# The opening's token sums and query weight sums on GpSimd, and query results turned by VectorE

## The chip, the cores and the metric

The kernel runs on one core of a Trainium2 chip. The metric is the device time of one execution in microseconds (us). Before the change three runs gave 1890.53, 1891.34 and 1893.8 us; the median is 1891.34.

## The reference

One decoder layer over 2048 tokens of width 1024, in float32. All branches start from one projection of the normed input:

```python
h = rms_norm(x, norm_g)
u = jnp.einsum('bsd,dc->bsc', h, w_in)
v_c, b_c, c_c, z_c, q, k, v, z_a, gate_logits = jnp.split(u, SPLIT_POINTS, axis=-1)
...
q = rms_norm(q.reshape(b, s, N_Q_HEADS, HEAD_DIM), q_norm_g)
k = rms_norm(k.reshape(b, s, N_KV_HEADS, HEAD_DIM), k_norm_g)
...
return x + jnp.einsum('bsd,de->bse', merged, w_out)
```

Branch A is a gated causal convolution of width 3, branch B a sliding-window attention (window 128, 16 query heads of 64 over 4 key heads) with sinks. The two are projected, merged with sigmoid gates and projected once more. For this change two things matter: the product of `h` with the query columns of `w_in`, and the mean square of each query head, which the norm of `q` needs.

## The kernel before, in words

The tokens are worked on in two tiles of 1024 (tile one is `t == 0`). Every projection is cut into units: two blocks of 128 columns by 1024 tokens, summed over 1024 inputs. Each float32 operand is held as a high and a low part, so a product of two operands takes three matmuls per pair of input chunks, twelve matmuls over the four pairs. ScalarE makes the high part (a cast), VectorE the low part (operand less high part).

**Units of seven products.** A unit (`sunit`, L494) does not form its eight block products one by one. It uses seven products of sums, in the order 1, 5, 6, 2, 7, 3, 4. The token operand of each is one of eight "forms" (`oph_m_j` in the order's rows: form m of input pair j, j from 0 to 3). Forms 1, 2, 3 and 8 are plain quarters of the normed input. Forms 5, 6, 7 and 4 are made of sums: `first_sum` overwrites the even chunk's left half (form 5), `second_sum` overwrites it again (form 6), `third` overwrites the even chunk's right half (form 7), `last_sum` writes a tile of its own, `t` (form 4). A sum may only overwrite what the form before has read, and a form may only be split after its sum. There are 16 such sums, of 128 x 512 elements, in the opening. The weights are treated in the same way (`sums`, L388): four sums per unit make the halves that products 5 and 6 (`wq_sh`, `wq_sl`) and 7 and 3 (`wq_th`, `wq_tl`) use, in place in the raw weights, after the plain half (`wq_ah`, `wq_al`) and the single (`wq_d`) have been split off. Product 6 adds onto a copy of product 1, which ScalarE writes into the bank Y (L503).

**The opening.** TensorE first makes keys and values by token, then the query units q0, q1, q2, q3, then the convolution's units. q0 has no sums: it uses forms 1, 2, 8 and 3 in plain products (`qunit`, L531), which gives VectorE time to make the others. q1 is the first unit with seven products.

**What a query result goes through** (`fin_q`, L808). A result is copied to `q_t`, scaled and split (`q_h`, `q_l`), and sent by GpSimd to memory in four transfers (`q2d`). For its mean square it is turned so that a head's elements lie along a row, squared by ScalarE, and summed up by VectorE. Where `BY_PE` holds a 1, TensorE turns it (`turn4`, the matmuls of L708: four transposes of 128 x 128 into a bank `ptq`) and the whole head lies in one row, 8 sums a result. Where it holds a 0, VectorE turns it in blocks of 32 x 32 into the bank (16 sums a result), and `squares_sum` adds the two halves of a head with four small copies and four small adds per unit. Before, q0, q1 and q2 of tile one are turned by TensorE and q3 by VectorE; in tile two VectorE turns all.

**What sets the order.** The order is written out in the program. `run` (L684) issues one product, then the work that `put` has placed at this tick: ScalarE's and VectorE's share of a weight piece, the steps of the tables `OP_X` to `OP_S`, results to evacuate. VectorE's instructions go through `vec`, a helper which also takes a step of waiting chains after each instruction, so all of them carry line L262. Each engine takes its own instructions strictly in order. GpSimd, besides, issues the transfers `vd` (values), `kd` (keys), `q2d` (queries), and later the attention's.

**The k transposes.** TensorE turns the normed keys of the first tile into banks `pbk` (L766), between products. These share a ring of three banks with `ptq`.

Of the kernel before, what the change touches and what calls it, by code (L numbers as in the profile page):

```python
# [60 lines left out]
Q_PARTS = [1, 4, 4, 0]  # L61
Q_SUMS = [8, 7, 6, 3]
ROOT = (1, 1, 1, 0)
BY_PE = [1, 1, 1, 0]
OP_X = [1, 1, 1, 6, 7, 7, 8, 11]
OP_P = [3, 2, 3, 4, 4, 4, 5, 6]
OP_L = [7, 8, 6, 6, 8, 7, 9, 7]
# [38 lines left out]
def block_kernel(  # L106
# [12 lines left out]
    nc = tc.nc  # L119
# [18 lines left out]
    def slot(shape, dt, name):  # L138
        return big.tile(shape, dt, tag="big", name=name)
# [160 lines left out]
    def add(o, a, b, eng=None):  # L300
        return (eng or vec).tensor_tensor(out=o, in0=a, in1=b, op=ALU.add)

    def sub(o, a, b, eng=None):
        return (eng or vec).tensor_tensor(out=o, in0=a, in1=b, op=ALU.subtract)
# [45 lines left out]
    def wpair(name):  # L350
        return [wpool.tile([P, KP * UC], F32R, tag="w", name=f"{name}{i}") for i in "hl"]

    def pieces_of(n):

        kind, srcs, key = plan[n]
        name = "w" + "_".join(str(i) for i in key)
        w = {}

        def two(hi, lo, src):
            return (lambda: nc.scalar.copy(hi, src),  # L362
                    lambda: vec.tensor_tensor(
                        out=lo, in0=src, in1=hi.bitcast(F32), op=ALU.subtract))

        if kind == "R":
            return w, []

        if kind:
            def pair(h, m1, m2, nm):  # L370
                hi, lo = (v.rearrange("p (i j c) -> p i j c", i=2, c=P) for v in wpair(f"{name}_{nm}"))
                for i, m in enumerate((m1, m2)):
                    w[m] = (hi[:, i], lo[:, i])
                return two(hi, lo, raws[2 * n + h])

            if kind == "P":
                return w, [(2, 1, lambda h=h: pair(h, (h, 0), (h, 1), f"p{h}")) for h in range(2)]

            def single():
                if n in paired:  # L380
                    hl = [slot([P, KP, P], F32R, f"{name}_d{i}") for i in "hl"]
                else:
                    d = wpool.tile([P, 2, KP, P], F32R, tag="w", name=f"{name}_d")
                    hl = [d[:, 0], d[:, 1]]
                w[4] = tuple(hl)
                return two(*hl, raws[2 * n + 1][:, 1])

            def sums():  # L388
                ra, rb = raws[2 * n], raws[2 * n + 1]

                def f():
                    sub(ra[:, 0], ra[:, 0], rb[:, 0])
                    summed.append(vec.chain(
                        lambda: add(rb[:, 0], rb[:, 0], rb[:, 1]),
                        lambda: sub(rb[:, 1], rb[:, 1], ra[:, 0]),
                        lambda: sub(ra[:, 1], ra[:, 1], rb[:, 1])))

                return (lambda: None, f)

            summed = []  # L400

            def of_sums(*args):
                summed[0]()
                return pair(*args)

            def single_sums():
                hi, lo = single()
                _, f = sums()

                def g():  # L410
                    lo()
                    f()

                return hi, g

            first = [(1, 0, single), (0, 0, sums)] if n not in paired else [(0, 0, single_sums)]
            return w, [(2, 0, lambda: pair(0, 1, 2, "a")), *first,
                       (2, 1, lambda: of_sums(1, 5, 6, "s")), (2, 1, lambda: of_sums(0, 7, 3, "t"))]
# [225 lines left out]
    def third(c, st):  # L644

        raw = st["raw"]
        sub(raw[c - 1, 1], raw[c, 1], raw[c - 1, 1])

    def norm_r(t, c, st):

# [2 lines left out]
    def first_sum(j, st):  # L653

        raw = st["raw"]
        sub(raw[2 * j, 0], raw[2 * j, 1], raw[2 * j, 0])

    def second_sum(j, st):

        raw = st["raw"]  # L660
        sub(raw[2 * j, 0], raw[2 * j + 1, 1], raw[2 * j, 0])

    def last_sum(j, st, to=None):

        raw = st["raw"]
        o = st.setdefault("t4", {})[j] = raw[2 * j, 0] if to is None else to
        sub(o, raw[2 * j + 1, 0], raw[2 * j, 0])

    def form(t, m, j, st):
        raw = st["raw"]  # L670
# [137 lines left out]
    def fin_q(t, j):  # L808
        by_pe = t == 0 and BY_PE[j]
        ss = small.tile([P, 32 if by_pe else 64], F32, tag="ss" if by_pe else "ss4", bufs=3 if by_pe else 2, name=f"qss{t}_{j}")  # L810
# [631 lines left out]
    for t in range(NT):  # L1442
# [9 lines left out]
        for word in (SEQ0, SEQ1)[t].split():  # L1452
            both_ = word.split("+")
            for name in both_:
                if len(both_) > 1:
                    paired.add(len(plan))
                key, j = name.rstrip("0123456789"), int(name[-1]) if name[-1].isdigit() else None
# [26 lines left out]
    raw, ops, xs = st["raw"], st["ops"], st["x"]  # L1484
# [77 lines left out]
    def t4(j):  # L1562
        last_sum(j, st, slot([P, H], F32, f"t4_{j}"))
# [24 lines left out]
    rights(0)  # L1588
    forms(1)
    each(0, lambda j: first_sum(j, st))  # L1590
    forms(2)
    rights(1)
    each(1, lambda j: second_sum(j, st))
    forms(3)
    forms(4)
    each(2, lambda j: third(2 * j + 1, st))
    forms(5)
    each(3, t4)
# [165 lines left out]
```

## Time and profile before

| | |
|---|---|
| runs | 1890.53, 1891.34, 1893.8 us |
| profiled execution | 1890.92 us, span 1889.2 us, clock 1.0 |
| TensorE busy | 1880.8 us |
| VectorE busy | 1540.0 us |
| ScalarE busy | 989.0 us |
| GpSimd busy | 728.7 us |

In the profile PE is TensorE (PEld its weight loads), DVE VectorE, ACT ScalarE, POOL GpSimd. A row of the order of time has the start and the length in us, engine, line, operation, what is written and read, and a count; square brackets tell what ended an idle time before it. A row by tile has the shortest, median and longest length in ns. A group's row has the busy time in all and the mean of one in ns. Matmuls overlap, so their pace is read from start to start. The difference between the execution and its span, 1.7 us, lies outside the program's instructions.

### The profile page before, as it was taken

The numbers are of one execution on the slowest core, as the hardware profiler recorded it, in microseconds if no ns is written. First come the engines' busy times: TensorE is split into PE (matmuls) and PEld (weight loads), VectorE is DVE, ScalarE is ACT, GpSimd is POOL, SyncE is SP. The second block draws the span as 40 slices with busy tenths as digits, with TensorE's granted clock in tenths as the row PEclk, the third lists the DMA queues.
The fourth block names the chain that finished last, engine by engine and source line by source line (L and its number), as shares of the span: only waits on it lengthen the run. The fifth ranks groups of instructions, "written<-read, shape, count | busy, mean of one in ns | idle before, by whom it ended". The sixth has DMA issues, their size and how long they took to land.

```text
span 1889.2 us, 27869 instructions
## 1 busy us (share of the span) xinstructions
PE 1880.8 (100%) x8638; PEld 1565.5 (83%) x8638; DVE 1540.0 (82%) x2536; ACT 989.0 (52%) x1993; POOL 728.7 (39%) x1038
## 2 busy tenths in 40 slices
PE   9999999999999999999999999999999999999999
PEld 7888888888888888888887888888888888888887
DVE  7989888789878889887579988888877789887654
ACT  7665554567665345435455645556566436344321
POOL 1472454456667111021075445656666311121000
PEclk9999999999999999999999999999999999999999
DMA  8475566689888978889367557768888869899653
GB/s 307 123 217 170 144 175 190 182 246 302 251 246 258 318 267 301 286 286 296 112 184 221 182 170 207 206 164 238 243 241 255 269 245 347 318 281 272 223 173 110
DMA packets 261189, 435.81 MB, mean 231 GB/s; under 512 B 33649, under 2 KB 124785, under 8 KB 261041
## 3 DMA queue, kind: packets, MB, share of 16 engines
q1 hardware_dynamic: 202848, 314.13, 50.3%
q0 software_dynamic: 58048, 119.87, 24.0%
q8 instruction: 69, 1.13, 0.3%
q14 instruction: 80, 0.65, 0.1%
q10 hardware_dynamic: 144, 0.03, 0.0%
HBM read 279.48 MB, written 154.42 MB: 230 GB/s over the span
## 4 chain that ended last, share of the span: by engine, by line
PE 82%; issue 7%; DVE 5%; DMA 3%; POOL 2%; ACT 1%; SPq 0%; POOLq 0%; DVEq 0%; ACTq 0%
PE Y L480 30%; PE Vcv L480 5%; PE Xcv L480 5%; PE po L1118 2%; PE Xgb L480 2%; PE Xb L480 2%; PE Vgb L480 2%; PE Xz L480 2%; PE Vb L480 2%; PE Vz L480 2%; PE Vo L480 2%; PE Xo L480 2%; PE Xza L480 2%; PE Vza L480 2%; PE Vga L480 2%
## 5 line engine op out<-in xcount | busy, mean ns | idle before, releaser
L1080 POOL DMA_DIRECT2D x<-fd x256 | 144.1, 614 | 69.7 <-DMA fd<-f 24.9
L1101 POOL TENSOR_SCALAR_AFFINE_SELECT xh<-xh 64x512 fp32r<-64x512 f32 x64 | 66.7, 1043 | 133.1 <-DVE xl L262 96.2
L1053 ACT ACTIVATE p<-s,st,rq 128x128 f32<-128x128 f32 x256 | 113.0, 451 | 5.7 <-DMA fd<-f 3.7
L1073 POOL DMA_DIRECT2D fd<-f x64 | 39.0, 610 | 176.6 <-DVE f L262 152.3
L480 PE MATMUL Xcv<-oph,wcv_ah 128*128 128x512 f32 x256 | 79.5, 392 | 0.0
L1134 POOL DMA_DIRECT2D od<-o x64 | 69.4, 1092 | 24.6 <-DMA od<-o 20.4
L855 POOL DMA_DIRECT2D q2d<-q_h x64 | 44.3, 692 | 84.3 <-ACT q_h L850 81.9
L1324 POOL DMA_DIRECT2D md<-thyb x32 | 27.4, 872 | 103.3 <-DVE thyb L262 87.7
L1101 POOL TENSOR_SCALAR_AFFINE_SELECT xl<-xl 64x512 fp32r<-64x512 f32 x64 | 64.3, 1004 | 4.4
L1101 POOL TENSOR_SCALAR_AFFINE_SELECT yp<-yp 64x512 fp32r<-64x512 f32 x64 | 55.7, 870 | 5.0 <-ACT yp L1088 0.9
L1101 POOL TENSOR_SCALAR_AFFINE_SELECT yp<-xl 64x512 fp32r<-64x512 f32 x64 | 56.1, 876 | 3.1
L480 PEld LDWEIGHTS Xcv<-oph,wcv_ah 128*128 128x128 f32 x256 | 47.3, 188 | 9.4
L262 DVE SCALAR_TENSOR_TENSOR y<-u,cols,y 128x512 f32<-128x512 f32 x64 | 51.5, 804 | 3.7 <-ACT y L1163 2.5
L262 DVE TENSOR_TENSOR p<-p,st 128x512 f32<-128x512 f32 x64 | 49.7, 776 | 2.6
L262 DVE TENSOR_TENSOR opa<-ina,opa 128x512 fp32r<-128x512 f32 x56 | 36.2, 686 | 18.3 <-ACT opa L297 18.3
L1053 ACT ACTIVATION_READ_ACCUMULATOR p<-s,st,rq 128x1 f32 x256 | 50.9, 199 | 0.0
L362 ACT CAST wcv_sh<-wcv_raw 128x1024 fp32r<-128x1024 f32 x16 | 16.8, 1053 | 63.5 <-DVE wcv_raw L262 63.5
L480 PE MATMUL Xcv<-oph,wcv_al 128*128 128x512 f32 x128 | 49.8, 389 | 0.0
L855 POOL DMA_DIRECT2D q2d<-q_l x64 | 44.1, 689 | 12.6 <-DVE q_l L262 9.9
L1028 PEld LDWEIGHTS s<-kq,q 128*128 128x128 f32 x256 | 45.9, 189 | 2.2
L262 DVE STREAM_TRANSPOSE f<-p 128x512 f32<-128x512 f32 x64 | 45.4, 710 | 2.7 <-DVE p L262 0.2
L262 DVE TENSOR_TENSOR opc<-inc,opc 128x512 fp32r<-128x512 f32 x56 | 36.1, 686 | 13.9 <-ACT opc L297 13.8
(774 smaller groups left out, 6611.5 us busy)
## 6 DMA issues: line engine op xcount, KB each, us to landing
wcv_raw<-in_w_in SPq DMA_DIRECT2D x32, 512.0 KB, 4.2
q<-q2d SPq DMA_DIRECT2D x64, 256.0 KB, 4.7
v<-vd SPq DMA_DIRECT2D x128, 128.0 KB, 4.7
fd<-f POOLq DMA_DIRECT2D x64, 256.0 KB, 3.8
x<-fd POOLq DMA_DIRECT2D x256, 64.0 KB, 3.6
gd<-th SPq DMA_DIRECT2D x64, 256.0 KB, 3.4
wq_raw<-in_w_in SPq DMA_DIRECT2D x16, 512.0 KB, 5.0
q2d<-q_h POOLq DMA_DIRECT2D x64, 128.0 KB, 3.7
```

The costliest lines, as they stand in the source:

```text
L262: r = f(*args, **kw)
L362: return (lambda: nc.scalar.copy(hi, src), lambda: vec.tensor_tensor(out=lo, in0=src, in1=hi.bitcast(F32), op=ALU.subtract))
L480: nc.tensor.matmul(ps, lhsT=w[:, j, :], rhs=b[:, m, :], start=start and j == 0 and i == 0, stop=j == KP - 1 and i == 2, skip_group_check=n ...
L855: nc.gpsimd.dma_start(q2d[t][j][half, q * 2 * HB : (q + 1) * 2 * HB, i, e, :], src[HALVES[e]].bitcast(F32).rearrange("p (b x) -> p b x", x ...
L1028: nc.tensor.matmul(sp[:, h, c, skip : 3 * HD], lhsT=q2[:, h, c, :], rhs=kq[:, 0, keys], start=False, stop=c == 1)
L1053: nc.scalar.activation(out=p[:, i, :], in_=sg[:, i, HD : 3 * HD], func=AF.Exp, bias=st[:, 1, i : i + 1], scale=rv[:, i // 2, i % 2 : i % 2 ...
L1073: nc.gpsimd.dma_start(fd, f)
L1080: nc.gpsimd.dma_start(x[QUADS[k]], src[k])
L1101: nc.gpsimd.affine_select(out=d4, in_=s4, pattern=[[0, 2], [-32 * sg, 2], [0, G], [-sg, 32]], compare_op=ALU.is_gt if prev else ALU.is_ge, ...
L1118: nc.tensor.matmul(po[:, cs], lhsT=v2[:, kind, :], rhs=xx[:, :, h * HD : (h + 1) * HD], start=h == 0 and n == 0, stop=n == 2, skip_group_c ...
L1134: put(tick[0] + ADD_WAIT, lambda: nc.gpsimd.dma_start(to, o[UH].rearrange("p c e q -> p (c e) q"), accum_op=ALU.add))
L1324: nc.gpsimd.dma_start(md[t][k, :, hs(q)], m, accum_op=ALU.add)
```

## The change

`BY_PE` becomes 0 for all four query units of tile one, so that VectorE turns their results. The sums on tokens in the opening (`first_sum`, `second_sum`, `third`, `last_sum`) and the four weight sums of q1, q2 and q3 are issued on GpSimd instead of VectorE. The weight sums of the other units stay on VectorE. No table of ticks changes. ScalarE's order up to product 6 of q1 is the same as before.

```diff
-BY_PE = [1, 1, 1, 0]
+BY_PE = [0, 0, 0, 0]
...
                 def f():
+                    if key[0] == "q" and key[1] == 0:
+                        eng = nc.gpsimd
+                        sub(ra[:, 0], ra[:, 0], rb[:, 0], eng)
+                        add(rb[:, 0], rb[:, 0], rb[:, 1], eng)
+                        sub(rb[:, 1], rb[:, 1], ra[:, 0], eng)
+                        sub(ra[:, 1], ra[:, 1], rb[:, 1], eng)
+                        summed.append(lambda: None)
+                        return
                     sub(ra[:, 0], ra[:, 0], rb[:, 0])
...
     def third(c, st):
-        sub(raw[c - 1, 1], raw[c, 1], raw[c - 1, 1])
+        sub(raw[c - 1, 1], raw[c, 1], raw[c - 1, 1], nc.gpsimd)
...
     def first_sum(j, st):
-        sub(raw[2 * j, 0], raw[2 * j, 1], raw[2 * j, 0])
+        sub(raw[2 * j, 0], raw[2 * j, 1], raw[2 * j, 0], nc.gpsimd)
...
     def second_sum(j, st):
-        sub(raw[2 * j, 0], raw[2 * j + 1, 1], raw[2 * j, 0])
+        sub(raw[2 * j, 0], raw[2 * j + 1, 1], raw[2 * j, 0], nc.gpsimd)
...
     def last_sum(j, st, to=None):
-        sub(o, raw[2 * j + 1, 0], raw[2 * j, 0])
+        sub(o, raw[2 * j + 1, 0], raw[2 * j, 0], nc.gpsimd)
```

GpSimd's queue before, from the first query result's last transfers to the third result's first; `xt` are the token chunks, `q_0_1_0` is query unit 0, block 1, token half 0:

```order
L855 DMA q2d_0_92<-q_0_0_0_l 64x8x64
L747 DMA vd<-v_4_765 64x4x128 x2
L747 DMA vd<-v_5_770 64x4x128 x2
L855 DMA q2d_0_92<-q_0_1_0_h 64x8x64
L855 DMA q2d_0_92<-q_0_1_0_l 64x8x64
L855 DMA q2d_0_92<-q_0_1_0_h 64x8x64
L855 DMA q2d_0_92<-q_0_1_0_l 64x8x64
L855 DMA q2d_0_92<-q_0_0_1_h 64x8x64
```

The same place after the change, as far as the second sum of pair two, in front of its form 6 (`xt_156` is the even chunk of pair zero, `xt_169` of pair two, `xt_176` of pair three; of two rows that read alike the first is the third sum, for form 7, the other the second sum, for form 6):

```order
L304 TENSOR_TENSOR xt_156<-xt_160,xt_156 128x512
L755 DMA vd<-v_4_765 64x4x128 x2
L755 DMA vd<-v_5_770 64x4x128 x2
L304 TENSOR_TENSOR xt_156<-xt_160,xt_156 128x512
L304 TENSOR_TENSOR t_1_792<-xt_165,xt_163 128x512
L863 DMA q2d_0_92<-q_0_1_0_h 64x8x64
L863 DMA q2d_0_92<-q_0_1_0_l 64x8x64
L863 DMA q2d_0_92<-q_0_1_0_h 64x8x64
L863 DMA q2d_0_92<-q_0_1_0_l 64x8x64
L304 TENSOR_TENSOR xt_169<-xt_172,xt_169 128x512
L304 TENSOR_TENSOR xt_176<-xt_179,xt_176 128x512
L304 TENSOR_TENSOR xt_169<-xt_172,xt_169 128x512
```

The token sums now stand between the transfers of values and queries, each of which waits for a split by VectorE. Ahead of this piece stand six token sums, the four weight sums of q1 and the four transfers of the first query result.

GpSimd's queue before, where the transfers of q1's last result end (`k_1_1` and `k_0_1` are parts of the keys):

```order
L855 DMA q2d_1_93<-q_1_1_0_h 64x8x64
L855 DMA q2d_1_93<-q_1_1_0_l 64x8x64
L776 DMA kd_100<-k_1_1_h 64x2x512
L776 DMA kd_100<-k_1_1_l 64x2x512
L776 DMA kd_100<-k_1_1_h 64x2x512
L776 DMA kd_100<-k_1_1_l 64x2x512
L776 DMA kd_100<-k_0_1_h 64x2x512
```

The same place after the change:

```order
L863 DMA q2d_1_93<-q_1_1_0_h 64x8x64
L863 DMA q2d_1_93<-q_1_1_0_l 64x8x64
L784 DMA kd_100<-k_1_1_h 64x2x512
L784 DMA kd_100<-k_1_1_l 64x2x512
L784 DMA kd_100<-k_1_1_h 64x2x512
L784 DMA kd_100<-k_1_1_l 64x2x512
L304 TENSOR_TENSOR wq_3_raw_892<-wq_3_raw_892,wq_3_raw_894 128x512
L301 TENSOR_TENSOR wq_3_raw_894<-wq_3_raw_894 128x512
L304 TENSOR_TENSOR wq_3_raw_894<-wq_3_raw_894,wq_3_raw_892 128x512
L304 TENSOR_TENSOR wq_3_raw_892<-wq_3_raw_892,wq_3_raw_894 128x512
L784 DMA kd_100<-k_0_1_h 64x2x512
```

The four weight sums of q3 stand behind 24 issues that follow the sums of q2: four `vd`, sixteen `q2d` of q1 and four `kd`.

VectorE's rows before, in front of the last forms 6 (product 6 of q1 reads them):

```order
L262 TENSOR_TENSOR xt_176<-xt_179,xt_176 128x512
L262 TENSOR_TENSOR xt_169<-xt_172,xt_169 128x512
L262 TENSOR_TENSOR xt_176<-xt_179,xt_176 128x512
L262 TENSOR_TENSOR oph_7_1_848<-xt_163,oph_7_1_848 128x512
L262 TENSOR_TENSOR oph_7_2_851<-xt_169,oph_7_2_851 128x512
L262 TENSOR_TENSOR t_2_854<-xt_172,xt_169 128x512
L262 SCALAR_TENSOR_TENSOR q_0_0_1_l<-q_0_0_1_t,gqk,q_0_0_1_h 128x512
```

And after:

```order
L262 TENSOR_TENSOR wq_1_sl<-wq_1_raw_302,wq_1_sh 128x1024
L262 TENSOR_TENSOR oph_7_1_848<-xt_163,oph_7_1_848 128x512
L262 TENSOR_TENSOR oph_7_2_851<-xt_169,oph_7_2_851 128x512
L262 SCALAR_TENSOR_TENSOR q_0_0_1_l<-q_0_0_1_t,gqk,q_0_0_1_h 128x512
L262 TENSOR_REDUCE kss_1_709<-ksq_3_828 128x8
```

The sums are gone from between the splits; what the splits read now comes from GpSimd.

## The prediction

> **What bounds the kernel now.** I read the page first, then the opening by stretches of 25 us.
>
> ```profile
> span 1889.2 us, 27869 instructions
> PE 1880.8 (100%) x8638; PEld 1565.5 (83%) x8638; DVE 1540.0 (82%) x2536; ACT 989.0 (52%) x1993; POOL 728.7 (39%) x1038
> 50.00:75.00 25.00, 25.00 (x112) 20.72 (x111) 24.65 (x45) 16.02 (x30) 7.94 (x12) 1.00 0.25 66
> 100.00:125.00 25.00, 25.00 (x125) 20.84 (x124) 19.92 (x36) 14.64 (x26) 18.40 (x29) 1.00 0.81 222
> ```
>
> TensorE never rests, so whatever it no longer does shortens the run and whatever makes it wait lengthens it. The second number of a stretch is TensorE's busy time, then the weight loads', VectorE's, ScalarE's and GpSimd's. VectorE is full at 50 to 75 us (24.65 of 25) and GpSimd has room (7.94); at 100 to 125 us it is GpSimd that is the busier of late (18.40), all of it the issuing of transfers. Next, TensorE's order of time, with and without a turn of a query result:
>
> ```profile
> 92.74 2.88 PE L480 MATMUL Y<-oph,wq_d 128*128 128x512 f32 x12
> 95.46 0.60 PE L708 MATMUL ptq<-ident,q_t 128*128 128x128 f32 x4
> 95.81 0.71 PE L480 MATMUL Xq<-oph,wq_ah 128*128 128x512 f32 x2
> 98.65 0.62 PE L480 MATMUL Vq<-oph,wq_sh 128*128 128x512 f32 x2
> 63.26 0.62 PE L545 MATMUL Qq<-oph,wq_p0h 128*128 128x512 f32 x2
> 79.94 1.03 PE L480 MATMUL Y<-oph,wq_sh 128*128 128x512 f32 x2
> 120.87 0.71 PE L480 MATMUL Vq<-oph,wq_sh 128*128 128x512 f32 x2
> ```
>
> A product of 12 matmuls alone takes 95.46 - 92.74 = 2.72 us, a turn with the product behind it 98.65 - 95.46 = 3.19. The last three rows are dates that I need: form 8 is first wanted at 63.26, form 6 at 79.94 (its first pair takes 0.32 longer than the 0.71 usual behind a transpose: it waits already now, for VectorE's forms), the weight sums of q2 at 98.65 and of q3 at 120.87.
>
> **Part 1: turns off TensorE.** 12 turns (three q units of four) at 3.19 - 2.72 = 0.47: **-5.6 us**. TensorE has no idle time for them to have hidden in. VectorE gets 12 transposes instead:
>
> ```profile
> 144.24 0.72 DVE L262 STREAM_TRANSPOSE ptq<-q_t 128x512 f32<-128x512 f32 x1
> L262 DVE TENSOR_TENSOR xt<-xt,xt 128x512 f32<-128x512 f32 x8 | 5.3, 675 | 0.0
> L262 DVE TENSOR_TENSOR wq_raw<-wq_raw,wq_raw 128x512 f32<-128x512 f32 x9 | 6.2, 685 | 0.1
> 50.10 1.28 DVE L262 TENSOR_TENSOR oph<-xt,oph 128x512 fp32r<-128x512 f32 x2
> 61.99 0.68 DVE L262 TENSOR_TENSOR oph<-xt,oph 128x512 fp32r<-128x512 f32 x1
> ```
>
> Instructions of 0.68 follow each other every 0.60 (1.28 for two), so the transposes cost VectorE 7.5 us, and the 28 sums that leave it (16 token, 12 weight) give back 16.8. The small copies and adds that replace four copies per unit are near even. This alone would be a gain.
>
> **Part 2: what a sum costs on GpSimd.** No row shows a two-input sum there. The nearest is the one-input select over the same 512 elements, and how it and VectorE treat each other:
>
> ```profile
> L1101 POOL TENSOR_SCALAR_AFFINE_SELECT xh<-xh x64: 742/764/1692, 188.9 to 1475.4; 64x512 fp32r<-64x512 f32 x64
> L262 DVE TENSOR_TENSOR p<-p,st x64: 691/692/1240, 166.2 to 1453.7; 128x512 f32<-128x512 f32 x64
> L262 DVE TENSOR_TENSOR y<-Xb,y x8: 678/683/692, 232.9 to 1323.7; 128x512 f32<-128x512 f32 x8
> 188.55 1.91 DVE L262 SCALAR_TENSOR_TENSOR y<-u,cols,y 128x512 f32<-128x512 f32 x2
> 188.85 1.07 POOL L1101 TENSOR_SCALAR_AFFINE_SELECT xh<-xh 64x512 fp32r<-64x512 f32 x1 [1.38 <-DVE xl L262]
> 189.99 1.07 POOL L1101 TENSOR_SCALAR_AFFINE_SELECT yp<-yp 64x512 fp32r<-64x512 f32 x1
> 167.56 1.50 DVE L262 SCALAR_TENSOR_TENSOR y<-u,cols,y 128x512 f32<-128x512 f32 x2
> ```
>
> Length: 0.74 for one input is the lower end, twice that, 1.48, the upper; I take the middle, **1.1**. Overlap: the two VectorE instructions at 188.55 take 1.91 where 167.56 shows 1.50, and the select starting inside the first takes 1.07, not 0.74: it waits 0.33 for that one, and then VectorE waits 0.4 for it. The next select takes 1.07 again. They alternate, one instruction at a time. Instructions with an operand in PSUM (y<-Xb,y, at most 692) never lengthen; those with both in SBUF do (p<-p,st, up to 1240). The opening's splits, norms and forms are all of the second kind. So a sum moved away frees 0.60 of VectorE and holds it up for 1.1.
>
> How far this goes for a longer instruction the rows leave open: the most that they show on one VectorE instruction is 1240 - 691 = 0.55. Were that the price of a sum, the six sums of the first stretch below would cost 3.3 in place of 6.6, what follows would start 3.3 sooner, and the time would be 1905. I take the whole 1.1, since the pair at 188.55 waited until the select had ended.
>
> [...]
>
> **Part 3: GpSimd's queue.** It works in order, and the sums stand between DMA issues that wait for VectorE.
>
> ```profile
> 47.50 2.48 POOL L747 DMA_DIRECT2D vd<-v  x4 [5.33 <-DVE v L262]
> 100.79 1.32 POOL L747 DMA_DIRECT2D vd<-v  x2 [9.04 <-DVE v L262]
> 103.63 0.70 POOL L855 DMA_DIRECT2D q2d<-q_h  x1
> 116.70 0.59 POOL L776 DMA_DIRECT2D kd<-k_l  x1
> 74.42 0.72 ACT L850 ACTIVATE q_h<-q_t,gqk 128x512 fp32r<-128x512 f32 x1
> 75.05 0.56 ACT L582 COPY q_t<-Qq 128x512 f32<-128x512 f32 x1
> 75.51 1.05 ACT L362 CAST wq_th<-wq_raw 128x1024 fp32r<-128x1024 f32 x1
> 76.46 1.66 ACT L297 CAST oph<-xt 128x512 fp32r<-128x512 f32 x3
> 78.02 0.58 ACT L503 COPY Y<-Xq 128x512 f32<-128x512 f32 x1
> 96.23 1.21 DVE L262 TENSOR_TENSOR wq_sl<-wq_raw,wq_sh 128x1024 fp32r<-128x1024 f32 x1
> ```
>
> A q2d issue takes 0.69, four vd 2.48, four kd 2.4. I walk the new order with these.
>
> Product 6 of q1. GpSimd is free at 49.98. VectorE's rows from 50.10 to the last form 8 (61.99 + 0.6) last 12.5, of which 2.4 are sums that left; six token sums hold it up for 6.6: it ends at 66.8 instead of 62.6, where TensorE wants it at 63.26 + 3 x 0.68 = 65.3 (1.5 late, in the next figure). The four weight sums of q1 alternate with VectorE and end at 72.6; four q2d issues 75.3; a token sum, behind the weight split on VectorE, 77.3; four vd 79.8; two sums 82.0; four q2d 84.7; one sum 85.85. Only now can ScalarE copy form 7 of pair two, and behind it stand q_h, q_t, the weight cast and three form-6 copies (at the pitch of the rows above 0.55 + 0.65 + 0.5 + 1.0 + 0.55 up to the first of the three, 89.1; the last waits until 90.4 for two further sums and ends at 91.0), then Y, 0.6, at 91.6. TensorE adds product 6 into that Y. It started in effect at 79.94 + 0.32 = 80.26 before: **+11.4**. VectorE has long caught up by then; what is late is GpSimd's queue, and ScalarE's behind it.
>
> Product 4 of q1 needs two more sums, which stand behind a sum, eight q2d (the later four wait for a split that VectorE reaches at 96.3) and four kd, so 103.7; the first of the two feeds TensorE at 103.9, and product 4 is wanted at 91.65 + 4 x 2.72 + 0.4 (a k transpose) = 102.9: **+1.0**.
>
> Product 5 of q2 needs the third weight sum: four kd and three sums behind that, 110.0, cast 1.0, split 1.2: lower half at 112.2, so a start at 111.75 (the lower half is first read 0.45 into a product). Wanted two products after product 4 began, at 103.9 + 5.44 = 109.35: **+2.4**.
>
> Product 5 of q3: the v transfers follow that weight split by 4.4 us (before, 97.44 to 100.79 is 3.35; a transpose and one more key row now stand ahead, 0.6 and 0.45). Then 24 DMA issues stand ahead of the third group of sums, which took 100.79 to 117.3 = 16.5 without a break. Then three sums 3.3, cast 1.0, split 1.2; and the bank of the k transposes in front of product 5 is now one that VectorE fills and reduces behind that split, 1.2 and 0.4. From 112.2 that is 140.2. Wanted at 111.75 + 7 x 2.72 + 0.8 (two k transposes) = 131.6: **+8.6**.
>
> Sum: 11.4 + 1.0 + 2.4 + 8.6 - 5.6 = **+17.8**. On the profiled execution, 1890.92 (span 1889.2 and 1.7 around it; the median of the runs is 1891.34, 0.4 more), that is **1908.7 us**. With 0.74 a sum, some 23 sums on this path give 8.3 back (1900); with 1.48 they add 8.7 (1917). VectorE keeps its 9 us of saved work all the same: they lie under GpSimd's chain and buy nothing.
>
> **The rivals.** *No exclusion for these sums.* The weight split of q1 is then over by 60 (62.6 less the 2.4 that left), and GpSimd's queue runs 60 + 4.4 + 2.8 + 1.1 + 2.5 + 2.2 + 2.8 + 1.1 = 76.9, ScalarE's chain ends at 81.7: product 6 is 1.5 late. Behind it three sums, eight q2d, eight kd, two and three sums put the third weight sum of q2 at 97.1, and product 5 of q2 at 98.85, close to its date. But the last step stays: from 98.85, 4.8 + 16.5 + 3.3 + 2.2 + 1.6 gives 127.2 for product 5 of q3 against 120.87, less the four turns behind it (1.9): +4.4, **1895.3**; with 0.74 a sum about +2, **1893**. For it: only one-input selects have been seen to exclude. Against: the excluded side is VectorE's two-input form, which is the same here.
>
> *GpSimd keeps up (the other side).* VectorE, 9 us lighter, delivers the v and q splits so early that the 24 issues are over before the third group is wanted. It decides at product 5 of q3: if the third sum ends by 113 (120.87 less 8 turns of 0.47, less cast, split, transpose and reduce), only part 1 is left: **1885.3**. Against: k's transposes and q1's results come from TensorE and are not sooner, and the second group of sums would have to end before 90. The change does do what it says: the order shows the 48 transposes gone from TensorE.
>
> **How the numbers follow.** A measurement of this kernel tells about 0.2% (3.8 us) from no change. Forecast with its ends of price (1900 to 1917): 0.81. No exclusion (1893 to 1895.3): 0.14, more than half of it within 0.2%. Keeps up (1885.3): 0.05. So faster 0.05, same 0.09, slower 0.86. The range takes in the first two cases, 1893 to 1917.
>
> **What would show it.** Sums on GpSimd of 1.1 alone and longer beside VectorE; VectorE's form rows at 51 to 76 us lengthened to 1.2 to 1.8; TensorE waiting for ScalarE's Y in front of product 6 of q1 (about 11 us) and for VectorE in front of the k transposes of q3 (about 8); no ptq on TensorE and no other wait of over 3 us. If GpSimd's third group ends before TensorE asks, or the waits in front of product 6 are under 3 us, the walk is wrong.

## The result, and the profile after

| | before | after |
|---|---|---|
| median of the runs | 1892.57 us (1890.53 to 1894.13, 4 runs) | 1918.92 us (1918.17 to 1919.58, 4 runs) |
| profiled execution | 1890.92 us | 1918.17 us |

The ratio is 1.0141, with a 95% interval of 1.0129 to 1.0153: 1.4% slower, 26.4 us by the medians and 27.25 us by the profiled executions. The forecast was 1908.7 us (+17.8), its range ended at 1917.

First the page of the kernel after: span and busy time of each engine, then four stretches of 25 us of the opening (length, TensorE, weight loads, VectorE, ScalarE, GpSimd, each with its count, then TensorE's granted clock, the DMA share and GB/s).

```profile
span 1916.4 us, 27810 instructions
PE 1883.0 (98%) x8590; PEld 1563.1 (82%) x8590; DVE 1550.7 (81%) x2523; ACT 991.5 (52%) x2005; POOL 772.5 (40%) x1066
75.00:100.00 25.00, 15.35 (x65) 12.25 (x64) 18.16 (x18) 10.59 (x18) 23.81 (x27) 0.80 0.50 139
100.00:125.00 25.00, 20.47 (x84) 14.99 (x83) 20.43 (x30) 13.34 (x23) 19.00 (x23) 1.00 0.60 168
125.00:150.00 25.00, 18.75 (x78) 15.18 (x77) 15.20 (x30) 11.81 (x25) 19.19 (x27) 0.86 0.65 183
150.00:175.00 25.00, 20.84 (x82) 16.10 (x81) 20.44 (x40) 13.35 (x26) 18.65 (x28) 0.93 0.75 216
```

TensorE lost its full occupation in the opening, nearly all of it from 75 to 175 us, and in three of these stretches its granted clock fell under 1.0 besides. VectorE's busy time went up (1540.0 to 1550.7), though 28 sums left it for 12 turns: its rows contain time in which it stands for GpSimd (two forms together take 3.48 at 64.03, beside GpSimd's sums, and 1.28 at 50.10 in the kernel before). Next, what TensorE waited for in the first 300 us (total, times, longest; the five largest), and five single rows of its order of time, at the dates that the prediction had worked out:

```profile
PE Vq L488 <- ACT q_t L590: 9.7, 1, 9.7
PE pbk L774 <- DVE qss L262: 6.3, 1, 6.3
PE Y L488 <- DVE q_t L262: 2.2, 1, 2.2
PE Y L488 <- DVE Vq L262: 2.1, 1, 2.1
PE Vcv L488 <- DVE wcv_sl L262: 1.9, 1, 1.9
```

```profile
92.03 0.70 PE L488 MATMUL Y<-oph,wq_sh 128*128 128x512 f32 x2
103.50 0.39 PE L488 MATMUL Y<-oph,wq_d 128*128 128x512 f32 x1
111.82 0.73 PE L488 MATMUL Vq<-oph,wq_sh 128*128 128x512 f32 x2
141.98 1.20 PE L488 MATMUL Vq<-oph,wq_sh 128*128 128x512 f32 x2
174.82 0.61 PE L488 MATMUL Xcv<-oph,wcv_ah 128*128 128x512 f32 x2
```

The first four are product 6 of q1 (forecast 91.6), product 4 of q1 (103.9), product 5 of q2 (111.75) and product 5 of q3 (140.2): the walk through GpSimd's queue was within 2 us up to here. The last row is product 2 of the first convolution unit. In the kernel before it stands here:

```profile
147.38 0.62 PE L480 MATMUL Xcv<-oph,wcv_ah 128*128 128x512 f32 x2
```

So it came 27.4 us late, which is the whole loss. From product 5 of q3 it was 26.5 us away before (120.87 to 147.38) and is 32.8 now: 6.3 us more, where the prediction reckoned 1.9 us less, four turns gone. That is where most of the missing 9.4 us (27.25 less 17.8) lies, and it is a stretch without any sum on GpSimd. What fills it are the waits for VectorE's `q_t` and `wcv_sl` (2.2 and 1.9) and matmuls at half the clock behind waits: product 5 of q3 takes 4.39 (2.81 before; the granted clock from 140 to 145 us is 0.50), and the convolution's products 5 and 6 take 2.0 more than before beside their wait (0.50 from 169.3 to 172.6). The three waits of about 2 us, for VectorE's `q_t`, `Vq` and `wcv_sl`, had no place in the prediction.

### The profile page after: what moved, and what is told of

Same layout as the page of the kernel before. It is cut to its first block, busy times and chain, and to the rows that moved or that the text cites. A ratio compares the mean times of both kernels' runs of the same rounds, so it can differ in the third digit from the quotient of the medians.

```text
span 1916.4 us, 27810 instructions
## 1 busy us (share of the span) xinstructions
PE 1883.0 (98%) x8590; PEld 1563.1 (82%) x8590; DVE 1550.7 (81%) x2523; ACT 991.5 (52%) x2005; POOL 772.5 (40%) x1066
## 4 chain that ended last, share of the span: by engine, by line
PE 83%; issue 6%; DVE 4%; POOL 4%; DMA 3%; ACT 1%; SPq 0%; POOLq 0%; DVEq 0%; ACTq 0%
PE Y L488 29%; PE Vcv L488 5%; PE Xcv L488 4%; PE po L1126 2%; PE Xb L488 2%; PE Xz L488 2%; PE Vb L488 2%; PE Vz L488 2%; PE Vo L488 2%; PE Xo L488 2%; PE Xza L488 2%; PE Vza L488 2%; PE Xgb L488 2%; PE Vya L488 2%; PE Vgb L488 2%
## 5 line engine op out<-in xcount | busy, mean ns | idle before, releaser
L1332 POOL DMA_DIRECT2D md<-thyb x32 | 27.4, 872 | 102.5 <-DVE thyb L262 80.4
L262 DVE TENSOR_TENSOR opa<-ina,opa 128x512 fp32r<-128x512 f32 x56 | 36.2, 687 | 17.9 <-ACT opa L297 17.8
```

The costliest lines, as they stand in the source:

```text
L262: r = f(*args, **kw)
L1332: nc.gpsimd.dma_start(md[t][k, :, hs(q)], m, accum_op=ALU.add)
```

## The experiments

Two theories stood at first. Q: the loss is GpSimd's queue as walked, and the turns are the small gain that was forecast. R: the waits for VectorE belong to the turns, which gain little or nothing. Each kernel is compared with the kernel before (medians 1891.52 to 1892.57).

### The parts alone: e1 to e4

e1 makes only the change of `BY_PE`. e2 has only the four token sums' helpers on GpSimd, e3 only the weight sums, e4 both kinds of sums, with the turns as before.

```diff
-BY_PE = [1, 1, 1, 0]
+BY_PE = [0, 0, 0, 0]
```

That is e1's edit of the kernel before; e4 is the kernel after with the line turned back.

e1, expected: 

> Only BY_PE becomes 0 0 0 0; all sums stay on VectorE. Theory Q (GpSimd's queue of sums and issues makes the loss, the turns are a gain of 12 x 0.47): 5.6 us faster than before, at most 1 us of it lost to a busier VectorE, so about -5 us and no wait of TensorE over 1 us between 75 and 180 us. Rival R (turning on VectorE is itself a loss: it makes the sums of Vq, the query splits and the convolution's weights late): the waits of 2.1, 2.2 and 1.9 us seen after the change stay, and the time is 0 to 5 us above before.

e2, expected: 

> Only the 16 token sums go to GpSimd; weight sums and turns stay as before. Theory Q: GpSimd's queue is shorter by the four weight sums of q1 (5.8 us in the walk), so product 5 or 6 of q1 is late by 5 to 6 us in place of 11.4 and product 4 by 1 to 3 more; nothing is late from q2 on: +7 to +9 us. If only VectorE's exclusion counted and not the queue, TensorE would wait for forms split by VectorE in q0 and q1 by 1 to 3 us, and not for ScalarE behind GpSimd.

e3, expected: 

> Only the weight sums of q1, q2 and q3 go to GpSimd; token sums and turns stay as before. Theory Q: q1 and q2 on time within 1 us, q3's third sum stands behind 24 issues and ends about 120.5, which makes product 5 of q3 2 to 4 us late: +2 to +4 us. If the queue of issues did not matter, +0 to +1.

e4, expected: 

> All sums on GpSimd as in the change, but q0, q1 and q2 are turned by TensorE as before. Theory Q: the change less its gain: 5.6 us more, less about 2 us for the bank wait in front of q3, so 1920 to 1923 us. Rival R: the waits for VectorE behind q2 go with the turns, and the time falls below the change's by 2 to 8 us: 1911 to 1917.

| kernel | median us | ratio, 95% interval | against before |
|---|---|---|---|
| e1 turns only | 1899.89 | 1.0041 [1.0029, 1.0054] | +8.3 |
| e2 token sums only | 1901.91 | 1.0055 [1.0042, 1.0069] | +10.3 |
| e3 weight sums only | 1899.85 | 1.0045 [1.0029, 1.0060] | +8.2 |
| e4 both sums | 1912.8 | 1.0111 [1.0098, 1.0125] | +21.2 |

The turns alone lose 8.3 us where -5.6 was forecast: that part of theory Q fell, and R's 0 to +5 was short of it too. The sums without the turns lose 21.2 us, R's figure; the prediction's terms for them add to 11.4 + 1.0 + 2.4 + 8.6 = 23.4. Each kind of sums alone costs more than was expected: e2 1.3 us over the range given (+7 to +9), e3 4.2 us (+2 to +4). The waits of e1, on TensorE:

```profile
PE pbk L766 <- DVE qss L262: 3.2, 1, 3.2
PE Y L480 <- DVE q_t L262: 2.2, 1, 2.2
PE Y L480 <- DVE Vq L262: 2.0, 1, 2.0
```

These are waits that the kernel after shows too, with no sum on GpSimd in this kernel.

In e3 the loss has two places. The first was not expected: in product 4 of q1 TensorE waits twice for VectorE's forms, 0.73 us each, and VectorE's four low parts there took 6.54 us while GpSimd worked on the weight sums of q2. From the start of product 4 of q1 to that of product 1 of q2 it is 5.34 us (92.67 to 98.01), 2.3 more than before (92.74 to 95.81).

```profile
90.49 6.54 DVE L262 TENSOR_TENSOR oph<-t,oph 128x512 fp32r<-128x512 f32 x4
95.40 0.96 PE L488 MATMUL Y<-oph,wq_d 128*128 128x512 f32 x3 [0.73 <-DVE oph L262]
```

The second is the one that the prediction named: VectorE stands in front of the weight split of q3 until ScalarE has cast what GpSimd, behind its DMA issues, has summed in the third group.

```profile
116.20 0.68 DVE L262 TENSOR_REDUCE qss<-ptq 128x8 f32<-128x512 f32 x1
124.22 1.32 DVE L262 TENSOR_TENSOR wq_sl<-wq_raw,wq_sh 128x1024 fp32r<-128x1024 f32 x1 [7.34 <-ACT wq_sh L362]
126.61 0.75 PE L488 MATMUL Vq<-oph,wq_sh 128*128 128x512 f32 x2
131.02 0.61 PE L488 MATMUL Y<-oph,wq_sh 128*128 128x512 f32 x2
```

TensorE waits 3.3 us for it, and product 5 of q3 then takes 131.02 - 126.61 = 4.41 where it took 2.81. The run's granted clock is 0.999 in the mean over its span of 1897.2 us, a loss of some 1.9 us; that it fell on this product is an estimate from these numbers. No later wait in the opening covers these 1.6 us.

### Place in the queue: e5

```diff
-                    if key[0] == "q" and key[1] == 0:
+                    if key[0] == "q" and key[1] == 0 and key[2] < 3:
```

This is e4 with the third group, q3's, back on VectorE. Expected: 

> As e4 (all the sums on GpSimd, the turns where they were), but the weight sums of unit q3 are VectorE's again; those of q1 and q2 stay on GpSimd. In e4 TensorE waited 4.7 us for VectorE's qss before the k transposes of q3, and product 5 of q3 then ran 4.00 instead of 2.82 us at the half clock. Theory Q (place in GpSimd's queue): the 24 DMA issues stand ahead of those four sums only, so both costs go: 4.7 + 1.2 = 5.9 us less than e4's 1912.8, 1906.9 (1905 to 1909), and the 12 us before product 5 of q1 stay. Rival C (the two engines slow each other at SBUF, the place in the queue does not matter): four sums of 20 back, some 1 us less, 1911 to 1913.

Measured: 1907.07 us, ratio 1.0082 [1.0069, 1.0096], against e4's 1912.8. Theory Q's 1906.9 is met, and no wait in front of the k transposes of q3 is left. Four sums behind 24 issues cost 5.7 us; C's 1 us is excluded. The clock is part of it: product 5 of q3 takes 3.99 us in e4 and 2.82 in e5, and the mean granted clock is 0.996 and 0.997.

### The half clock: e6

Behind its long wait (9.65 and 5.69 us) TensorE ran slow in the kernel after and in e2: a pair of product 5's matmuls took 1.06 and 1.05, where 0.62 is usual. e6 is e2 with product 1 of q1 computed three times, so that TensorE works where it waited.

```diff
+        if key == ("q", 0, 1):
+            for again in range(2):
+                hi, lo = ready[u][1]
+                for j in range(KP):
+                    b = ops[1][j]
+                    for i, (w, m) in enumerate(((hi, 0), (hi, 1), (lo, 0))):
+                        nc.tensor.matmul(
+                            xb, lhsT=w[:, j, :], rhs=b[:, m, :],
+                            start=j == 0 and i == 0, stop=j == KP - 1 and i == 2)
         product(xb, u, 1, ops, True)
```

Expected: 

> As e2 (only the token sums on GpSimd), but the twelve matmuls of product 1 of q1 run three times in a row into the same bank (the first two results are overwritten), 24 x 0.227 = 5.44 us of TensorE work in what was its 5.7 us wait behind them. In e2 the granted clock stood at 0.5 for 6.83 us after that wait and product 5 and the next two took 5.09 and 3.02 instead of 2.73 and 2.85, and the whole came to +10.3 us. Theory T (the lower clock follows the wait, and costs time of its own): the clock stays at 1.0, the products after it take 2.7 to 2.9, and the time falls by 2.4 us, to 1899.5 (1898.5 to 1900.5), though more work is done. Rival L (the products after the wait are slow for late operands, the clock does not matter): 1901.9 or up to 5 us more.

Measured: 1901.59 us, ratio 1.0054 [1.0041, 1.0066], e2's time (1901.91). The granted clock of the profiled execution is 1.0 in the mean (0.998 in e2), the wait for `q_t` shrank to 0.2 us, and nothing was gained:

```profile
PE Y L480 <- DVE oph L262: 1.8, 1, 1.8
```

Product 6 now waits for VectorE's form. T's time is missed and L's is met, though T was right about the clock, which follows the wait: the time that slow matmuls took there was covered by the next late operand. At this place the half clock is a symptom and no term of the sum. Behind the wait in front of q3 it is a term, as the traces of e3 to e5 show (product 5 of q3 takes 4.41 and 3.99 in e3 and e4, and 2.82 in e5, without that wait); no wait that came later in the opening of e3 and e4 covered it.

### Why the turns cost: e7, e8, e11, e12

e7 is e1 with VectorE's turns written to SBUF in tile one's units, e8 moves q2's turns alone; first e7's edit, then e8's.

```diff
-                    pt = mbank(f"pt{nm}")
+                    pt = slot([P, HB, P], F32, f"pt{nm}")
                     vec.transpose(out=pt.rearrange("p b q -> p (b q)"), in_=qt)
```

```diff
-BY_PE = [1, 1, 1, 0]
+BY_PE = [1, 1, 0, 0]
```

e7, expected: 

> As e1 (only the turns moved to VectorE, +8.3 us), but VectorE writes each turned half in the opening's units to a slot in SBUF in place of one of the three banks that the k transposes share. Theory B (the banks: a turn holds one from VectorE's turn to VectorE's late sum, and the k transposes of q3 wait for it): the 3.2 us wait of the k transposes and the half clock behind it (product 5 of q3 at 4.42) go, the waits for q_t and Vq stay: 4 to 5 us less, 1895 to 1896. Theory V (VectorE is late with everything after 105 us, the bank is only where it shows): the wait turns up at the next thing that VectorE owes, 1899 to 1901.

e8, expected: 

> As the kernel before, but of the three units whose turns the change moves only q2's go to VectorE; q0's and q1's stay TensorE's, and no sum moves. TensorE loses 4 x 0.43 = 1.7 us of work. Theory V (it is the turns beside VectorE's full stretch from 87 to 125 us that cost, q0's and q1's): the waits for Vq and before the k transposes of q3 do not come up, and the time is the kernel before's less 0 to 1.7 us, 1890 to 1892. Rival U (each unit's turns cost alike, a third of 8.3): +2.8, 1894.4.

e7 measured 1898.59 us (1.0036 [1.0023, 1.0050]), 1.3 us less than e1: the wait in front of the k transposes went, and the one for `q_t` grew from 2.2 to 4.2 us. That is nearer to V (1899 to 1901) than to B (1895 to 1896): the bank is mostly where lateness shows. e8 measured 1896.78 us (1.0024 [1.0015, 1.0034]): +5.1 us for q2's four turns alone, more than either theory gave. In the profiled execution only 3.1 us of it stand in the opening, near U's 2.8; the first row is the kernel before, the second e8:

```profile
251.33 0.66 PE L480 MATMUL Xcv<-oph,wcv_ah 128*128 128x512 f32 x2
254.42 0.66 PE L480 MATMUL Xcv<-oph,wcv_ah 128*128 128x512 f32 x2
```

Another 2.8 us come from short waits between 453 and 840 us, far from the edit; whether the edit causes them is not shown. So e8 alone does not tell VectorE's work for four turns (4 x 0.63 = 2.5 us; 0.63 is from a turn's start at 139.88 to the next row's at 140.51 in the kernel after) from a further cause. What ScalarE waited for from 84 to 165 us pointed to one; first e1, then the kernel before:

```profile
ACT ptq L782 <- DVE ptq L262: 18.9, 13, 4.7
```

```profile
ACT ptq L782 <- DVE ptq L262: 4.2, 3, 1.7
```

One such place in e1, in ScalarE's order of time:

```profile
95.47 0.58 ACT L782 ACTIVATE ptq<-ptq 128x512 f32<-128x512 f32 x1 [4.72 <-DVE ptq L262]
95.97 0.59 ACT L582 COPY q_t<-Vq 128x512 f32<-128x512 f32 x1
96.44 1.05 ACT L362 CAST wq_sh<-wq_raw 128x1024 fp32r<-128x1024 f32 x1
```

The square of a turned result sits in ScalarE's queue right behind the turn. In the kernel before no square waited for a turn of TensorE there, and three waited for q3's turns by VectorE (the 4.2 us above); VectorE's turn comes when VectorE gets to it, and ScalarE stands for it with the copies of products, the weight casts and the halves `q_h` behind. VectorE needs those casts and halves and becomes late itself. e11 and e12 take this away: the square comes one step of the product loop later, in e11 on top of e7 and in e12 on top of e8.

```diff
-                sq = head_square(pt, nm)
-                put(tick[0] + 1, lambda: reduce(sq))
+                if t == 0 and not by_pe:
+                    put(tick[0] + 1, lambda: square(pt))
+                else:
+                    square(pt)
+
+            def square(pt):
+                sq = head_square(pt, nm)
+                put(tick[0] + 1, lambda: reduce(sq))
```

e11, expected: 

> As e7 (only the turns moved to VectorE, written to SBUF), but ScalarE's square of each turned half is issued one step of the product loop (2.7 us) after VectorE's turn in place of right behind it, and the sum of squares a step after that. Theory H (the hand-over: ScalarE works in order, and the square that it used to get from TensorE now makes it stand for VectorE's turn while the copies of products and the halves of q stand behind; in e7 it waited 15.7 us for turns from 84 to 165 us): those waits fall under 5 us, TensorE's wait of 4.2 us for q_t goes, and the time falls by 4 to 8 us, to 1891 to 1894. Theory W (VectorE's own work of 0.63 us for each turn, and what it makes late, is the whole cost): VectorE does the same work, so 1897 to 1900.

e12, expected: 

> As e8 (only q2's turns moved to VectorE, +5.1 us; the turns go to the shared banks), with ScalarE's square of q2's and q3's turned halves one step after VectorE's turn. Theory H: ScalarE's waits for turns (7.3 us from 84 to 165 us, 4.2 in the kernel before) fall under 4 us, the 1.9 us wait for q_t, the 0.7 us wait for wcv_sl and the half clock between them go, and the time comes to the kernel before's less what TensorE saves: 1890 to 1892. Theory W: 1896 to 1898.

e11 measured 1892.65 us (before 1892.53; ratio 0.9999 [0.9990, 1.0009]), 5.9 us under e7 with the same work on each engine, within H's range. e12 measured 1893.88 us (1.0010 [1.0000, 1.0019]), 2.9 us under e8 and 2 us over what H gave. W is excluded twice. ScalarE's squares waited for turns 15.7 us in e7 and wait 0.4 in e11, again from 84 to 165 us:

```profile
ACT ptq L782 <- DVE ptq L262: 15.7, 11, 4.7
```

```profile
ACT ptq L782 <- DVE ptq L262: 0.4, 1, 0.4
```

VectorE's sum of squares comes a step later too, but in that stretch of e7 VectorE waited for no square; what it waited for was ScalarE's halves `q_h` (5.3 us, 2.1 in e11) and `k_h` (2.8, none listed in e11).

e11 still isn't faster than the kernel before, though TensorE has 12 turns less. Its waits for VectorE in the opening's units show where they went:

```profile
PE Vcv L480 <- DVE wcv_sl L262: 1.9, 1, 1.9
PE Y L480 <- DVE Vq L262: 1.5, 1, 1.5
PE Y L480 <- DVE q_t L262: 1.2, 1, 1.2
PE Y L480 <- DVE Vcv L262: 0.7, 1, 0.7
```

1.9 + 1.5 + 1.2 + 0.7 = 5.3 us of new waits for VectorE, against 5.6 us saved.

### Putting it together, and the queue once more: e13, e14

e13 is the kernel after with e11's two edits. e14 is e2 with q0's splits and issues later:

```diff
-Q_PARTS = [1, 4, 4, 0]
+Q_PARTS = [7, 4, 4, 0]
```

e13, expected: 

> The whole change (all sums on GpSimd, all turns by VectorE), with what e11 had: tile one's turned halves go to SBUF and ScalarE's square of each comes one step of the product loop after VectorE's turn. Theory S (the losses are two things apart, GpSimd's queue for the sums and the hand-over for the turns): the turns' part goes and the sums' part stays, 1918.9 less 7.2 (what e1 lost to e11), 1911.7 (1910 to 1914, about e4's 1912.8), with the waits before product 5 of q1 (some 9.7 us) and before the k transposes of q3 (4 to 5 us) still there. Rival M (with ScalarE free of the hand-over, the sums' waits shrink too, since ScalarE's own queue made them long): under 1908.

e14, expected: 

> As e2 (only the token sums on GpSimd, +10.3 us), with the splitting of q0's results and their 16 DMA issues on GpSimd put six steps of the product loop later (7 for 1), so that ten of the token sums that stood among or behind them come first in GpSimd's queue; ScalarE's and VectorE's halves of q0 move along. Theory Q (the place in the queue: 8 to 12 issues of 0.69 us and a 2.65 us wait for q_l stand ahead of the sums that form 7 needs): ScalarE's 7.6 us wait for a sum, TensorE's 5.7 us wait before product 5 of q1 and the half clock go, and the time falls to 1892 to 1896. Rival C (the sums are slow because they run beside VectorE, 1.6 to 1.75 us each): the queue's order changes little, 1899 to 1903.

e13 measured 1915.54 us (1.0123 [1.0110, 1.0136]): 3.4 us less than the kernel after, not 7.2. The sums' part stays, so M is out, and S's 1910 to 1914 is missed by 1.5. The two losses don't simply add. TensorE's wait in front of q3's product 5 is now 4.3 us for the weight cast that stands for GpSimd's third group, so part of what the later square frees is waited out for GpSimd. The rest is lost in the convolution's first unit: e13 begins product 5 there at 161.36, ahead of e4 (162.56), waits 1.9 us for VectorE's `wcv_sl`, and begins product 6 at 167.96, behind e4 (165.28): 6.60 for product 5, 4.70 without the wait, where 2.72 is usual. Behind the same wait in the kernel after the granted clock is 0.50 (169.3 to 172.6 us). Why VectorE is late there was not tried.

e14 measured 1903.8 us (1.0066 [1.0054, 1.0078]): no gain on e2, 0.8 over C's range, and theory Q is wrong for the token sums. ScalarE's longest wait for a token sum fell (7.6 to 3.5 us), and TensorE's for `q_t` from 5.7 to 1.0, but another took its place:

```profile
PE Vq L480 <- DVE wq_sl L262: 4.1, 1, 4.1
```

GpSimd's and VectorE's order of time at that point:

```profile
73.96 1.31 POOL L304 TENSOR_TENSOR xt<-xt,xt 128x512 f32<-128x512 f32 x1
75.22 1.28 POOL L304 TENSOR_TENSOR t<-xt,xt 128x512 f32<-128x512 f32 x1
76.46 4.96 POOL L304 TENSOR_TENSOR xt<-xt,xt 128x512 f32<-128x512 f32 x4
81.39 1.25 POOL L304 TENSOR_TENSOR t<-xt,xt 128x512 f32<-128x512 f32 x1
```

```profile
73.28 10.45 DVE L262 TENSOR_TENSOR wq_sl<-wq_raw,wq_sh 128x1024 fp32r<-128x1024 f32 x1
```

One weight split, 1.21 us long in the kernel before, lasted 10.45: it stood for the whole series of seven sums, and ended 1.09 us after the last of them. In e2 DMA issues stand between the sums, and the same split took 2.28. The token sums cost this time either way, as a place in GpSimd's queue or as a stop of VectorE.

## Why the prediction was wrong

**The step that failed is part 1**: "12 turns (three q units of four) at 3.19 - 2.72 = 0.47: -5.6 us", and for VectorE's side of it "This alone would be a gain". The saving on TensorE is real (12 x 0.47), but the part has no row for who takes the turned result next. e1 measured +8.3 in place of -5.6. Of this swing of 13.9 us, 8.2 are gone in e11 (+8.3 to +0.1 against the kernel before): the smaller share with the banks (e7), the larger with ScalarE's standing for VectorE's turns. The rest is VectorE late with `wcv_sl`, `Vq`, `q_t` and `Vcv`, the 5.3 us of waits that e11 keeps. In the whole change the turns cost 6.1 us (e4's 1912.8 to 1918.92), of which e13's two edits take 3.4 back.

**The exclusion** held, in a stronger form than "they alternate, one instruction at a time". Form rows were lengthened as forecast, for instance in the kernel after:

```profile
64.03 3.48 DVE L262 TENSOR_TENSOR oph<-xt,oph 128x512 fp32r<-128x512 f32 x2
69.14 0.67 DVE L262 TENSOR_REDUCE kss<-ksq 128x8 f32<-128x512 f32 x1
70.52 1.78 DVE L262 TENSOR_TENSOR oph<-xt,oph 128x512 fp32r<-128x512 f32 x1
```

The sum of squares between them, with one input, keeps its 0.67 (0.67 in the kernel before). Nor did the instruction that started first get done first: e14's split is on record from 73.28, 0.68 us ahead of the first sum, and all seven sums went by before it was done, at 83.73.

**The price of a sum**, 1.1, was low: alone it took 1.30 and 1.26 in the kernel after, beside VectorE 1.6 to 1.75 in most single rows, with the waiting in it, and 6.21 for the first three.

```profile
133.56 1.30 POOL L304 TENSOR_TENSOR wq_raw<-wq_raw,wq_raw 128x512 f32<-128x512 f32 x1
134.94 1.26 POOL L301 TENSOR_TENSOR wq_raw<-wq_raw 128x512 f32<-128x512 f32 x1
```

**The queue.** The four dates came within 2 us (+11.4, +1.0, +2.4 and +8.6 were worked out from them), and the sums together cost 21.2 us where 23.4 stood. Some of this is luck: steps of the walk missed both ways and cancelled. The sum behind the first four `q2d` was given 2.0 us and took 1.3, the two behind the `vd` were given 2.2 and took 3.1. And product 5 of q2 began at the date forecast by another road: TensorE came to it late already, since product 4 of q1 was 5.3 us long for VectorE's late forms. It then waited 0.64 for the weight split, which was done at 113.1 (112.2 said) and would have held it anyway.

```profile
105.94 1.66 PE L488 MATMUL Y<-oph,wq_d 128*128 128x512 f32 x6 [0.71 <-DVE oph L262]
113.20 0.50 PE L488 MATMUL Vq<-oph,wq_sl 128*128 128x512 f32 x1 [0.64 <-DVE wq_sl L262]
```

The wait at q1 (9.7 us, about 11 said) showed one product earlier than said: product 5 needs a bank that ScalarE frees with a copy standing behind the same late form cast.

```profile
85.40 0.62 ACT L297 CAST oph<-xt 128x512 fp32r<-128x512 f32 x1 [11.00 <-POOL xt L304]
86.55 0.56 ACT L590 COPY q_t<-Qq 128x512 f32<-128x512 f32 x1
```

For q3 the mechanism was right (e3, e5): a wait of 6.3 us in the kernel after where about 8 was said, and 5.7 us by e5, which has the turns on TensorE, where 8.6 stood. For q1 the queue alone was not the cause, since e14 takes ten token sums out from behind the issues and the loss stays, now as a stop of VectorE.

**"VectorE keeps its 9 us of saved work all the same"** was wrong too: its busy time rose by 10.7 us, and the turns found it late. Both rivals fell: the exclusion is there, and GpSimd did not keep up.

## What to carry to other kernels

When work moves to another engine, price the hand-over as well as the work: list whose queue the next step sits in and what stands behind it there. If an engine in order now has to wait for a slower producer, put the consumer a step later before judging the move; here that was worth 5.9 us at the same work with the turns alone; in the whole change it was worth, together with the banks, 3.4. A sum sent to GpSimd was no sum saved here: it freed 0.60 us of VectorE, and VectorE's forms of 0.68 took up to 1.78 beside it, in single rows of the kernel after. DMA issues in GpSimd's queue ahead of the sums delayed them (24 issues, 5.7 us, by e5); without issues between them the sums stopped VectorE (one split of 1.21 us lasted 10.45, in e14).

## What the runs showed of the hardware

- A VectorE instruction with both inputs in SBUF, the weight split of e14, was not done until a series of seven sums on GpSimd was over: 10.45 us for 1.21. The other way round, a GpSimd sum took 4.63 us in e3 while six VectorE rows of 0.69 went by, none of them lengthened (the next took 1.79):

```profile
60.41 4.63 POOL L304 TENSOR_TENSOR wq_raw<-wq_raw,wq_raw 128x512 f32<-128x512 f32 x1 [11.03 <-ACT k_n L737]
```

- TensorE's granted clock halved in or behind some waits: in the kernel after it stands at 0.5 for 10.24, 6.83 and 3.41 us, three, two and one times 3.41, at waits of 9.65, 6.25 and 1.90. A matmul behind the 9.65 us wait takes 0.63 at first and 0.40 later, though its bank and operands are the same kind:

```profile
87.16 1.22 PE L488 MATMUL Vq<-oph,wq_sh 128*128 128x512 f32 x2 [9.65 <-ACT q_t L590]
88.18 0.63 PE L488 MATMUL Vq<-oph,wq_sl 128*128 128x512 f32 x1
90.73 0.40 PE L488 MATMUL Vq<-oph,wq_sl 128*128 128x512 f32 x1
```

e6, which fills the wait of 5.69 us in front of product 5 of q1, has a mean granted clock of 1.0 where e2 has 0.998. The length of a wait alone does not tell: the third stretch at half the clock goes with a wait of 1.90 us, while behind the wait of 2.08 us at 121 us the clock stays at 1.00 (121 to 128 us). What decides between the two these runs do not show.
